# Rotating 96 images by 90 degrees: smaller first and last pieces, and first loads split over two queues

## Chip, cores and metric

The kernel runs on one core of a Trainium2 chip. The metric is the device time of one execution in microseconds (us); lower is better.

## The reference

```python
batch, c, h, w = 32, 3, 256, 256
x = np.random.randn(batch, c, h, w).astype(np.float32)

def reference(x):
    return np.rot90(x, k=1, axes=(-2, -1)).astype(np.float32)
```

Each of the 32 x 3 = 96 images of 256 x 256 float32 values (256 KB) is rotated by a quarter turn: a transposition of the image and a reversal of the order of its rows. All 25.17 MB are read once and 25.17 MB are written once; there is no arithmetic.

## The kernel before

The 96 images are taken in 6 groups of 16 (4.19 MB). A group goes through three stages:

- Two loads of 2 MB each on the sync queue (SP, line L43, queue q1 in the profile) fill a tile S of 128 partitions with 2 x 4096 float32 values each. A partition holds, for each half of the group, R = 16 whole rows of an image.
- Sixteen transposes on VectorE (DVE, L49) move S to a tile U. Each works on blocks of 32 x 32 values and handles one column offset q out of 16: 512 values per partition. The reversed strides in the source view do the reversal. The 32 columns of a block are made of 16 column positions times the 2 halves of the group, so every transpose reads both loads, and all 16 are needed before either half of U is complete.
- Two stores of 2 MB each on the scalar queue (ACT, L51, queue q10) write U to the output.

```python
src = S.rearrange("p b (r k q) -> p q r k b", r=R, q=R)[:, ::-1, :, ::-1]
dst = U.rearrange("p a (q k r) -> p q r k a", q=R, r=R)
for q in range(R):
    nc.vector.transpose(dst[:, q], src[:, q])
```

S and U come from pools of three buffers each. The loop over the groups is written out when the kernel is built, and the framework puts the semaphores in: a load of group 3 waits until the transposes of group 0 have read its buffer, a transpose of group 3 until group 0's stores have left U. Each transfer signals one of eight DMA semaphores, which are used again in turn; a transfer that takes one again waits for the transfer that had it before. Each queue issues its transfers in the order of the program. SP only issues loads, and ACT only issues stores; DVE only transposes.

Of the kernel before, what the change touches and what calls it, by code (L numbers as in the profile page):

```python
# [1 line left out]

# [4 lines left out]


@with_exitstack
def kernel(  # L10
    ctx: ExitStack,
    tc: tile.TileContext,
    x: bass.AP,
    out: bass.AP,
):
    nc = tc.nc
    B, C, H, W = x.shape
    assert H == W == 256
    N = B * C
    P = 128  # L20
    R = 16
    K = H // R
    A = 32 // K
    G = 4 * A * A
    F = R * W
    fp32 = mybir.dt.float32


    x_v = x.rearrange("b c h w -> (b c h w)").rearrange(
        "(g b a qk f) -> g b qk a f", b=A, a=A, qk=4 * K, f=F  # L30
    )

    o_v = out.rearrange("b c h w -> (b c h w)").rearrange(
        "(g b a qk f) -> g a qk b f", b=A, a=A, qk=4 * K, f=F
    )

    in_pool = ctx.enter_context(tc.tile_pool(name="in_pool", bufs=3))
    out_pool = ctx.enter_context(tc.tile_pool(name="out_pool", bufs=3))

    for g in range(N // G):  # L40
        S = in_pool.tile([P, A, F], fp32, name="S")
        for b in range(A):
            nc.sync.dma_start(out=S[:, b], in_=x_v[g, b])  # L43
        U = out_pool.tile([P, A, F], fp32, name="U")

        src = S.rearrange("p b (r k q) -> p q r k b", r=R, q=R)[:, ::-1, :, ::-1]
        dst = U.rearrange("p a (q k r) -> p q r k a", q=R, r=R)
        for q in range(R):
            nc.vector.transpose(dst[:, q], src[:, q])  # L49
        for a in range(A):  # L50
            nc.scalar.dma_start(out=o_v[g, a], in_=U[:, a])  # L51


# [1 line left out]
_INS = ['x']  # L55
_OUTS = [((32, 3, 256, 256), 'float32')]


# [23 lines left out]
```

## Time and profile before

| | |
|---|---|
| Time, median of 3 runs (lowest to highest) | 124.6 us (124.37 to 124.67) |
| Profiled execution: time, span | 124.52 us, 122.7 us |
| VectorE busy, 96 transposes | 90.7 us, 74% of the span |
| Bytes read and written in HBM | 25.17 MB and 25.17 MB |
| Mean DMA rate over the span | 410 GB/s |
| q1 (loads), q10 (stores), share of the 16 DMA engines | 48.9%, 47.9% |
| 12 loads of 2,048 KB, issue to landing | median 22.3 us |
| 12 stores of 2,048 KB, issue to landing | median 23.3 us |

The span runs from the first to the last instruction of the core, and the time of an execution is some 1.8 us longer. In the profile, rows of slices show how busy an engine is in each fortieth of the span, as a digit in tenths. A line such as "q1 hardware_dynamic" gives a queue's packets, its megabytes and the share of the 16 DMA engines' time that its packets took. The time from issue to landing includes the wait behind earlier transfers of the same queue. SPq and ACTq are the queues that issue DMAs.

### The profile page before, as it was taken

The numbers are of one execution on the slowest core, as the hardware profiler recorded it, in microseconds if no ns is written. First come the engines' busy times: TensorE is split into PE (matmuls) and PEld (weight loads), VectorE is DVE, ScalarE is ACT, GpSimd is POOL, SyncE is SP. The second block draws the span as 40 slices with busy tenths as digits, with TensorE's granted clock in tenths as the row PEclk, the third lists the DMA queues.
The fourth block names the chain that finished last, engine by engine and source line by source line (L and its number), as shares of the span: only waits on it lengthen the run. The fifth ranks groups of instructions, "written<-read, shape, count | busy, mean of one in ns | idle before, by whom it ended". The sixth has DMA issues, their size and how long they took to land.

```text
span 122.7 us, 182 instructions
## 1 busy us (share of the span) xinstructions
DVE 90.7 (74%) x96; POOL 0.2 (0%) x4
## 2 busy tenths in 40 slices
DVE  0000699999999999999999999999906999930000
POOL 0000000000000000000000000000000000000000
DMA  3999999999999999999999999999999999999992
GB/s 85 406 433 443 427 427 427 427 427 427 310 432 432 433 433 427 427 433 432 419 433 438 427 427 427 432 438 432 432 427 438 438 427 433 433 427 427 427 432 101
DMA packets 3457, 50.34 MB, mean 410 GB/s; under 512 B 384, under 2 KB 384, under 8 KB 384
## 3 DMA queue, kind: packets, MB, share of 16 engines
q1 hardware_dynamic: 1728, 25.17, 48.9%
q10 hardware_dynamic: 1728, 25.17, 47.9%
q14 instruction: 1, 0.01, 0.0%
HBM read 25.17 MB, written 25.17 MB: 410 GB/s over the span
## 4 chain that ended last, share of the span: by engine, by line
DMA 53%; DVE 31%; SPq 1%; issue 1%; DVEq 1%; ACTq 0%
DVE U L49 31%; DMA out_dram<-U 28%; DMA S<-in_x_dram 26%; SPq L43 1%; DVEq L77 1%; ACTq L51 0%; DVEq L49 0%
## 5 line engine op out<-in xcount | busy, mean ns | idle before, releaser
L49 DVE STREAM_TRANSPOSE U<-S 128x512 f32<-128x512 f32 x96 | 90.7, 1055 | 17.7 <-DMA S<-in_x_dram 13.3
L66 POOL MEMSET const-uint8-127<- 128x1 uint8 x1 | 0.1, 102 | 0.0
L66 POOL MEMSET const-bfloat16-1.0<- 128x1 bf16 x1 | 0.1, 101 | 0.0
L66 POOL MEMSET const-float32-0.0<- 128x1 f32 x1 | 0.1, 98 | 0.2 <-issue 0.2
L66 POOL MEMSET const-float32-1.0<- 128x1 f32 x1 | 0.1, 98 | 0.0
## 6 DMA issues: line engine op xcount, KB each, us to landing
S<-in_x_dram SPq DMA_DIRECT2D x12, 2048.0 KB, 22.3
out_dram<-U ACTq DMA_DIRECT2D x12, 2048.0 KB, 23.3
```

The source lines that it names most:

```text
L43: nc.sync.dma_start(out=S[:, b], in_=x_v[g, b])
L49: nc.vector.transpose(dst[:, q], src[:, q])
L66: nc = _bacc.Bacc("TRN2", target_bir_lowering=False, num_devices=1)
L77: with _tile.TileContext(nc) as tc:
```

## The change

The kernel still takes six groups of 16 images, with the same pools, and groups 1 to 4 are handled as before (lines L64, L69 and L71 in the changed kernel). The first and the last group are of another kind: each is made of 4 pieces of 4 images (1 MB).

- A partition holds R = 8 rows of one image per piece, that is 2048 values or 8 KB. 32 partitions hold a whole image, so a piece can be transposed without the others.
- One transpose instruction (L53) with an 8 x 8 x 32 access pattern does a whole piece, and one store of 1 MB (L54, scalar queue) follows it.
- The last group's pieces are loaded by one transfer each on the sync queue (L48).
- The first group's pieces are loaded by two transfers each: partitions 0 to 63 on the sync queue (L45) and partitions 64 to 127 on the scalar queue (L46), 512 KB each.

```diff
-    R = 16
-    K = H // R
-    A = 32 // K
-    G = 4 * A * A
-    F = R * W
+    G = 16
+    KINDS = [1, 2, 2, 2, 2, 1]
+    F = G * H * W // P
...
-    for g in range(N // G):
-        S = in_pool.tile([P, A, F], fp32, name="S")
-        for b in range(A):
-            nc.sync.dma_start(out=S[:, b], in_=x_v[g, b])
-        U = out_pool.tile([P, A, F], fp32, name="U")
+    for g, kind in enumerate(KINDS):
+        S = in_pool.tile([P, F], fp32, name="S")
+        U = out_pool.tile([P, F], fp32, name="U")
+        if kind == 1:
...
+            R = 8
+            Sv = S.rearrange("p (s f) -> p s f", s=4)
+            Uv = U.rearrange("p (s f) -> p s f", s=4)
+            xv = xf[g].rearrange("(s p f) -> s p f", s=4, p=P)
+            ov = of[g].rearrange("(s p f) -> s p f", s=4, p=P)
+            for s in range(4):
+                if g == 0:
+                    nc.sync.dma_start(out=Sv[:64, s], in_=xv[s, :64])
+                    nc.scalar.dma_start(out=Sv[64:, s], in_=xv[s, 64:])
+                else:
+                    nc.sync.dma_start(out=Sv[:, s], in_=xv[s])
+            for s in range(4):
...
+                src = Sv[:, s].rearrange("p (r k q) -> p q r k", r=R, q=R)[:, ::-1, :, ::-1]
+                dst = Uv[:, s].rearrange("p (q k r) -> p q r k", q=R, r=R)
+                nc.vector.transpose(dst, src)
+                nc.scalar.dma_start(out=ov[s], in_=Uv[:, s])
+        else:
...
+            R = 16
...
+            for b in range(2):
+                nc.sync.dma_start(out=Sv[:, b], in_=xv[b])
...
+            for q in range(R):
+                nc.vector.transpose(dst[:, q], src[:, q])
+            for a in range(2):
+                nc.scalar.dma_start(out=ov[a], in_=Uv[:, a])
```

More of the change, by code (lines that the diff above doesn't have):

```diff
@@ L20 @@
     P = 128
-    R = 16
-    K = H // R
-    A = 32 // K
-    G = 4 * A * A
-    F = R * W
-    fp32 = mybir.dt.float32
[L29 to L35, printed above, removed]
+    G = 16
+    KINDS = [1, 2, 2, 2, 2, 1]
+    assert len(KINDS) * G == N
+    F = G * H * W // P
+    fp32 = mybir.dt.float32
@@ L37 @@
+    xf = x.rearrange("b c h w -> (b c h w)").rearrange("(g f) -> g f", g=N // G)
+    of = out.rearrange("b c h w -> (b c h w)").rearrange("(g f) -> g f", g=N // G)
     in_pool = ctx.enter_context(tc.tile_pool(name="in_pool", bufs=3))
     out_pool = ctx.enter_context(tc.tile_pool(name="out_pool", bufs=3))
-    for g in range(N // G):
-        S = in_pool.tile([P, A, F], fp32, name="S")
-        for b in range(A):
-            nc.sync.dma_start(out=S[:, b], in_=x_v[g, b])
-        U = out_pool.tile([P, A, F], fp32, name="U")
[L46 to L51, printed above, removed]
+    for g, kind in enumerate(KINDS):
[20 more added lines that the diff above has]
+            R = 16
+            Sv = S.rearrange("p (b f) -> p b f", b=2)
+            Uv = U.rearrange("p (a f) -> p a f", a=2)
+            xv = xf[g].rearrange("(b a qk f) -> b qk a f", b=2, a=2, f=F // 2)
+            ov = of[g].rearrange("(b a qk f) -> a qk b f", b=2, a=2, f=F // 2)
+            for b in range(2):
+                nc.sync.dma_start(out=Sv[:, b], in_=xv[b])
+            src = Sv.rearrange("p b (r k q) -> p q r k b", r=R, q=R)[:, ::-1, :, ::-1]
+            dst = Uv.rearrange("p a (q k r) -> p q r k a", q=R, r=R)
+            for q in range(R):
+                nc.vector.transpose(dst[:, q], src[:, q])
+            for a in range(2):
+                nc.scalar.dma_start(out=ov[a], in_=Uv[:, a])
```

## The prediction

> **What bounds the kernel now.** I read four views, in this order: the slices of the page, the DMA answer for stretches of the trace, the same stretches as a table of windows, and the groups of instructions with their waits. The slices say which resource is full:
>
> ```profile
> DVE  0000699999999999999999999999906999930000
> ...
> DMA  3999999999999999999999999999999999999992
> GB/s 85 406 433 443 427 427 427 427 427 427 310 432 432 433 433 427 427 433 432 419 433 438 427 427 427 432 438 432 432 427 438 438 427 433 433 427 427 427 432 101
> DMA packets 3457, 50.34 MB, mean 410 GB/s; under 512 B 384, under 2 KB 384, under 8 KB 384
> ```
>
> VectorE (DVE) starts in the fifth slice and ends four slices before the end. The 16 DMA engines are busy in all slices but the ends, at 427 to 438 GB/s whatever they do. Three things fall short: the first slice (85), one in the middle (310, about 31 to 34 us) and the last (101). Who was on the engines, for 2 to 30, 36 to 90 and 93 to 118 us:
>
> ```profile
> q1 hardware_dynamic: 800, 11.80, 100.2%
> ...
> q1 hardware_dynamic: 793, 11.68, 50.6%
> q10 hardware_dynamic: 790, 11.63, 50.3%
> ...
> q10 hardware_dynamic: 739, 10.80, 100.8%
> ```
>
> q1 is the sync queue (loads), q10 the scalar queue (stores). Loads alone, an even mixture and stores alone all fill the engines. So moving stores earlier buys no rate by itself; what can be bought is time in which the engines are short of work. The windows price it (columns: stretch, length, DVE, POOL, clock, DMA share, GB/s):
>
> ```profile
> 0.00:3.00 3.00, 0.00 (x0) 0.20 (x4) 1.00 0.34 87
> ...
> 30.00:33.00 3.00, 3.00 (x4) 0.00 (x0) 1.00 0.99 333
> 33.00:36.00 3.00, 3.00 (x5) 0.00 (x0) 1.00 0.91 377
> 36.00:90.00 54.00, 52.81 (x57) 0.00 (x0) 1.00 1.01 432
> ```
>
> Against 432 GB/s, the start loses 3 x (1 - 87/432) = 2.4 us. The middle loses 3 x (1 - 333/432) + 3 x (1 - 377/432) = 0.69 + 0.38 = **1.07 us**. Payload at 432 is 50.33 MB / 432 = 116.5 us of the 122.7 us span; most of the rest is start and end latency, which no order of groups removes. In the middle dip the DMA share is 0.99 and 0.91, while the rate is down by a quarter and an eighth: packets took longer, the engines were not short of packets. It coincides with the first stores and with the first refill of S, both issued at 28.58 us:
>
> ```profile
> 28.58 1.19 SPq L43 DMA_DIRECT2D S<-in_x_dram  x2
> 28.58 1.45 ACTq L51 DMA_DIRECT2D out_dram<-U  x2
> ```
>
> DVE's size, from the timeline, is 15.20 us for a group of 16 transposes, 0.95 us each (the page's mean of 1055 ns includes overlap with the next):
>
> ```profile
> 93.14 15.20 DVE L49 STREAM_TRANSPOSE U<-S 128x512 f32<-128x512 f32 x16 [4.15 <-DMA out_dram<-U]
> ```
>
> A group costs the DMA engines 8.39 MB / 432 = 19.4 us. DVE has 4 us to spare in each.
>
> [...] No transfer of the kernel before covers half the partitions on the SBUF side[...].
>
> **The change, part by part.** Durations are of the profiled execution: span 122.7, time 124.52, so 1.82 us outside the span; it lies 0.08 under the median of 124.6, which I neglect.
>
> 1. *Issue.* The order of the built program has on the sync queue 4 half loads (L45), 8 loads of 2 MB (L64) and 4 of 1 MB (L48); on the scalar queue 4 half loads (L46) ahead of the stores: 4 of 1 MB, 8 of 2 MB, 4 of 1 MB. That is 36 DMAs for 24. An issue takes 0.6 us (604 ns median for loads). The scalar queue's 4 extra end near 0.7 + 2.4 = 3.2 us, before any store is ready; cost 0, covered by the wait for data. If that cover were gone they would delay the first store by 2.4 us.
>
> 2. *First store.* The first 2 MB landed 7.6 us after issue at 0.73, so 1 MB would land 2.4 us sooner, at about 5.9 us. Transposing a piece (L53, 128x2048) at 0.95 us per 512 elements takes 3.8 us: the first store is issued near 9.7 us, not 28.58. DVE's total stays 96 x 0.95 = 91.2 us. The 8x8x32 form isn't in the trace; bounds follow in the rivals.
>
> 3. *Does either queue run dry?* Loads alone move 3.2 MB up to 9.7 us. Then group 0's stores, in 8 KB packets against the loads' 16 KB, get a third: 4.19 MB in 29 us, to 38.8 us, with 8.4 MB loaded. Group 1 is loaded near 28 us and transposed 15.2 us later, so q10 is empty from 38.8 to 43.4 us, and loads take the whole rate (2.0 MB). The other 11.6 MB of loads share evenly, 54 us, to about 97 us. Group 3's first load waits for S of group 0, free near 20 us, and later refills for a group transposed long before. Semaphores are reused, so a load now also waits for an older transfer: group 3's second load for group 0's third store (about 31 us), group 5's third piece for group 2's first store (about 73 us). Both times q1 still holds over 2 MB, as group 2 and group 4 are still arriving. Cost 0. At 97 us 9.3 MB of stores remain, 21.5 us, while DVE needs about 12 us and the last store 2.4: the end stays full.
>
> 4. *The dip.* If it was the refill meeting a nearly drained queue, it goes: -1.07. If it is what the first stores cost whenever they come, it moves to 10 us: 0. I take -0.5.
>
> 5. *Packets of 8 KB.* Groups 0 and 5 have 1,024 more packets, 64 per engine. An 8 KB instruction fetch (q14) in a stretch of 0.4 us had a share of 4.8%: 0.048 x 16 x 0.4 = 0.307 us. A 16 KB packet is 1.008 x 16 x 25 / 659 = 0.612 (10.80 MB are 659 packets). So the overhead of one more packet is between 0 and 0.008 us: 0 to 0.5 us in sum, I take 0.25. Twelve more DMAs add 12 semaphore packets per engine, 0.1 us at a packet's 0.008.
>
> 6. *The halves.* Group 0's 4.19 MB normally take 9.7 us. Both queues hold equal bytes[...]. [...] I take the middle, **+4.85**, and keep 0 and +9.7. What sits behind it: group 1's loads behind the lower halves on q1, group 0's stores behind the upper halves on q10[...]. The loss is paid in full, because later stages have no spare DMA time. A gain below 0 is limited to quicker start-up from two issuers, under the 0.4 us that 3 to 6 us lose at 377 GB/s (another row of the windows).
>
> Sum: 124.52 - 0.5 + 0.25 + 0.1 + 4.85 = **129.2 us**.
>
> **The rivals.** *A: the halves complement each other and the dip goes.* For it: [...] q1 and q10 together already ran at 432. [...] Time: 124.52 - 1.07 + 0.35 - 0.3 (start) = 123.5, **faster**. It decides if the half stage runs above 400 GB/s: below that, 4.19/0.4 - 9.7 = 0.8 us eats the gain. *B: [...] the dip moves to 10 us.* 124.52 + 0.35 - 0.3 = 124.6, no change; the page's high DMA share in the dip speaks for slow packets at the first store, not for an empty queue. *C: strict serialization*, +9.7: 134.1[...]. *D: the new transpose form is slow.* [...] DVE starts group 5 near 93 us and must end by 117 for the end to stay full, so 6 us per piece is where it decides; at twice the known rate, 7.6 us, it ends 4 x 1.6 = 6.4 us late: 131. [...] *E: the change doesn't advance the stores.* If the scalar queue's halves lag, store 0 leaves late, up to 22 us in case C; still no dry queue, so it costs nothing of its own.
>
> **How the numbers follow.** A measurement of this kernel tells about 0.3% (0.37 us) from no change. Halves held back (the forecast through C): 0.60. A: 0.15. B: 0.22, of which 0.02 falls on slower. D: 0.03. So faster 0.15, same 0.20, slower 0.65. For slower cases alone the range is 125.5 to 134. The whole range runs from 123.9, inside A, to 133.9, just short of strict serialization; about 1 in 6 is left out.
>
> **What would show it.** Right: in the first 12 to 22 us the rate is clearly under 430 with a high DMA share (8 KB packets taking over 0.31 us each), the last half load lands after 14 us, later slices stay at 427 to 438, and DVE's first instruction is near 6 to 8 us. Step 4 shows as a dip near 10 us or none; step 2 as the first L54 issue; step 3 as no slice under 420 from 40 us on. Wrong: a rate of 430 from 4 us on, or a long idle end with DVE as the last releaser.

## The result, and the profile after

The changed kernel takes 131.62 us (median of 4 runs, 131.33 to 132.75) against 124.56 us for the kernel before (4 runs): a ratio of 1.0585, 95% interval 1.052 to 1.065. It is slower by 7.1 us, where 129.2 was forecast, inside the range. The profiled execution took 131.33 us with a span of 129.5 us.

The slices of the page of the changed kernel (3.24 us each), and its queues:

```profile
DVE  0047698930099999999999999079999999574000
...
DMA  3999999999999999999999999999999999999993
GB/s 91 223 233 253 256 250 362 422 433 420 435 420 453 422 443 415 450 410 435 450 410 433 445 415 430 435 435 410 448 425 430 420 440 420 453 435 397 425 428 137
DMA packets 4673, 50.34 MB, mean 389 GB/s; under 512 B 576, under 2 KB 576, under 8 KB 576
```

The DMA engines look as busy as before in every slice, but in the second to sixth they move only 223 to 256 GB/s. After that the rate is what it was. The deep dip in the eleventh slice before (310) has no counterpart. VectorE now starts in the third slice and has gaps; none of them matters, because the DMA engines have work all the way (share 1.01 to 1.02 from 3 to 117 us).

The windows (stretch, length, DVE busy, POOL busy, clock, DMA share, GB/s), first of the kernel after, then of the kernel before:

```profile
0.00:3.00 3.00, 0.00 (x0) 0.20 (x4) 1.00 0.23 60
3.00:21.00 18.00, 10.81 (x3) 0.00 (x0) 1.00 1.02 249
21.00:36.00 15.00, 5.66 (x3) 0.00 (x0) 1.00 1.01 429
36.00:90.00 54.00, 49.71 (x54) 0.00 (x0) 1.00 1.01 430
90.00:117.00 27.00, 24.54 (x15) 0.00 (x0) 1.00 1.02 433
```

```profile
3.00:21.00 18.00, 7.67 (x9) 0.00 (x0) 1.00 0.99 422
21.00:36.00 15.00, 15.00 (x17) 0.00 (x0) 1.00 0.99 404
```

As lost time against 432 GB/s (length x (1 - rate/432)): from 3 to 21 us 7.6 us after and 0.4 us before; from 21 to 36 us 0.1 and 1.0. The difference is +7.2 and -0.9. The other stretches add some 0.5, which makes the 6.8 us by which the spans differ.

What the packets did, from the DMA answer for 4 to 16 us of the kernel after (queue, packets, MB, share of 16 engines):

```profile
DMA packets 448, 2.91 MB, mean 242 GB/s; under 512 B 93, under 2 KB 93, under 8 KB 93
...
q10 hardware_dynamic: 238, 1.58, 55.9%
q1 hardware_dynamic: 210, 1.33, 45.8%
```

Of 448 packets 93 are under 512 B (the page has 576 of these for 36 transfers, 16 each; the prediction calls them semaphore packets); the other 355 are rows of 8 KB. The engines' time, 1.017 x 16 x 12 us, over 355 gives 0.55 us a row. In e1_full_sync, without the split, it is 0.31 (4 to 9 us: 1.023 x 16 x 5 us over 264 rows). The engines count as busy, but each row takes them longer. The two queues share about evenly.

The new transpose form is nearly as dear per element as the old one (group row: busy us, mean ns, idle before and what ended it):

```profile
L53 DVE STREAM_TRANSPOSE U<-S 128x2048 f32<-128x2048 f32 x8 | 31.4, 3957 | 13.5 <-DMA S<-in_x_dram 13.5
```

3,957 ns for 2,048 values per partition is 0.99 us for 512, against 0.95 of the old form.

### The profile page after: what moved, and what is told of

It is laid out like the page before. It is cut to its first block, busy times and chain, and to the rows that moved or that the text cites. A ratio compares the mean times of both kernels' runs of the same rounds, so it can differ in the third digit from the quotient of the medians.

```text
span 129.5 us, 183 instructions
## 1 busy us (share of the span) xinstructions
DVE 91.9 (71%) x72; POOL 0.2 (0%) x4
## 3 DMA queue, kind: packets, MB, share of 16 engines
q1 hardware_dynamic: 2048, 23.07, 45.0%
## 4 chain that ended last, share of the span: by engine, by line
DMA 63%; DVE 25%; issue 1%; ACTq 1%; SPq 0%; DVEq 0%
DMA S<-in_x_dram 48%; DVE U L69 22%; DMA out_dram<-U 15%; DVE U L53 3%; ACTq L46 1%; SPq L48 0%; DVEq L69 0%
## 5 line engine op out<-in xcount | busy, mean ns | idle before, releaser
L69 DVE STREAM_TRANSPOSE U<-S 128x512 f32<-128x512 f32 x64 | 60.6, 1052 | 12.8 <-DMA S<-in_x_dram 12.6
L53 DVE STREAM_TRANSPOSE U<-S 128x2048 f32<-128x2048 f32 x8 | 31.4, 3957 | 13.5 <-DMA S<-in_x_dram 13.5
```

The costliest lines, as they stand in the source:

```text
L53: nc.vector.transpose(dst, src)
```

## The experiments

The theory (P), an assumption of the author that the runs were to try: what counts is which partitions a transfer covers. When all of them lie in the lower half (0 to 63) or all in the upper half (64 to 127), it runs at little over half rate: 249 GB/s in the changed kernel from 3 to 21 us, 422 in the kernel before. Rivals: the small pieces and packets cost the time (Q), two queues that load at once disturb each other (T), any transfer of 64 partitions or 512 KB is slow (R). Diffs are against the changed kernel unless said otherwise.

**e1_full_sync: the split undone, pieces kept.**

```diff
-                if g == 0:
-                    nc.sync.dma_start(out=Sv[:64, s], in_=xv[s, :64])
-                    nc.scalar.dma_start(out=Sv[64:, s], in_=xv[s, 64:])
-                else:
-                    nc.sync.dma_start(out=Sv[:, s], in_=xv[s])
+                nc.sync.dma_start(out=Sv[:, s], in_=xv[s])
```

> Only the split is undone: group 0's four pieces are loaded by one 128-partition transfer each, on the sync queue. Theory P [...]: the rate from 3 to 12 us is back at 420 GB/s or more and the time falls by the 7.2 us that the half stage lost, to 124.1 +- 0.4 us. Rival Q (small pieces, 8 KB packets or the new order of stores cost the time): it stays above 129 us. For the middle dip: if it was what the first stores cost whenever they come, a slice near 10 us falls to about 310 GB/s and the time is 124.6 or more; if it was the late refill, no slice falls and the time is 123.7 to 124.2.

Measured: 124.08 us, 0.9961 of the kernel before (0.9948 to 0.9973). P holds and Q falls: the split alone costs 7.5 us, and the pieces by themselves gain 0.45. Windows of this kernel:

```profile
3.00:21.00 18.00, 15.44 (x4) 0.00 (x0) 1.00 1.02 421
21.00:36.00 15.00, 8.28 (x9) 0.00 (x0) 1.00 1.00 424
```

```profile
12.00:15.00 3.00, 3.00 (x2) 0.00 (x0) 1.00 1.00 366
```

The first stretch is back at 421. The finer window has 366 GB/s just after the first store was issued at 9.45 us. The time fits the late refill (123.7 to 124.2), but the rate does fall after the first store, though not to 310. So this run left the dip open.

**e2_full_two_queues: full width, but two queues.**

```diff
-                    nc.sync.dma_start(out=Sv[:64, s], in_=xv[s, :64])
-                    nc.scalar.dma_start(out=Sv[64:, s], in_=xv[s, 64:])
+                if g == 0 and s % 2:
+                    nc.scalar.dma_start(out=Sv[:, s], in_=xv[s])
```

> Group 0's pieces are loaded by one 128-partition transfer each, pieces 0 and 2 on the sync queue, 1 and 3 on the scalar queue: two queues load at once, but no transfer covers half the partitions. Theory P: full rate from 3 us, time within 0.5 us of the kernel with all four on the sync queue. Rival T (two queues that load at the same time disturb each other, whatever the partitions): 240 to 300 GB/s in the first 20 us and 129 us or more.

Measured: 123.93 us, 0.9956 (0.9941 to 0.9972), the fastest kernel of all, though its interval overlaps that of e1_full_sync. While both queues load, it runs at 420 GB/s:

```profile
3.00:12.00 9.00, 3.58 (x1) 0.00 (x0) 1.00 1.00 420
```

e1_full_sync has 424 in the same window. T falls: two queues that load at once do no harm here.

**e3_halves_sync: halves, but one queue.**

```diff
-                    nc.scalar.dma_start(out=Sv[64:, s], in_=xv[s, 64:])
+                    nc.sync.dma_start(out=Sv[64:, s], in_=xv[s, 64:])
```

> The halves are kept, but all eight transfers of group 0 are on the sync queue, lower half, upper half, and so on. Theory P: [...] the rate is 216 to 225 GB/s (two queues gave 249 from 3 to 21 us), group 0 takes about 19 us and the time is 133 to 134.5 us, slower than the changed kernel. Rival T (two queues loading): with one queue the loss is gone, 124 to 125 us.

Measured: 131.56 us (1.0574, 1.0552 to 1.0595), the same as the changed kernel and not 133 or more. Its windows say why the rate was as expected and the total was not:

```profile
3.00:18.00 15.00, 8.39 (x3) 0.00 (x0) 1.00 1.02 221
18.00:21.00 3.00, 3.00 (x1) 0.00 (x0) 1.00 0.98 344
```

One queue runs at 221 GB/s, slower than two at 242 (4 to 16 us above), as the author had estimated. But the scalar queue is free of loads here, so its first store (issued at 11.96 us, with packets on q10 only from 18 us on) runs beside the last half loads: q10 moved 0.61 MB from 18 to 21 us and the rate rose to 344. In the changed kernel the stores stand behind the scalar queue's half loads: its first store, issued at 12.19 us, landed 18.0 us later, here it took 12.6. The losses from 3 to 21 us come out alike, 7.9 and 7.6 us. The expectation had left that filling out.

**e4_before_halves: the split alone, on the kernel before.**

```diff
-            nc.sync.dma_start(out=S[:, b], in_=x_v[g, b])
+            if g == 0:
+                xh = x_v[g, b].rearrange("(h qk) a f -> h qk a f", h=2)
+                nc.sync.dma_start(out=S[:64, b], in_=xh[0])
+                nc.scalar.dma_start(out=S[64:, b], in_=xh[1])
+            else:
+                nc.sync.dma_start(out=S[:, b], in_=x_v[g, b])
```

> The kernel before with one part of the change alone: each of its first two 2 MB loads is split by partition halves over the sync and scalar queues (1 MB each, 16 KB packets); groups, transposes and stores are as before. Theory P: 4.19 MB at 220 to 290 GB/s instead of 430, 5 to 9 us more than before: 130 to 134 us, 16 KB packets of 0.9 to 1.2 us in that stage. Rival Q (small pieces or packets): 124.6 us, as before.

Measured: 133.98 us, 1.0766 (1.0732 to 1.0799): 9.45 us more than before, where 5 to 9 was expected; the time is within its 130 to 134. Two windows of this kernel:

```profile
3.00:24.00 21.00, 0.00 (x0) 0.00 (x0) 1.00 1.00 225
36.00:90.00 54.00, 53.85 (x58) 0.00 (x0) 1.00 1.00 418
```

From 3 to 24 us it moves 225 GB/s where the kernel before moves 424. Group 0's 4.19 MB at half of 432 GB/s would cost 9.7 us more, so with two queues and 16 KB packets the loss is nearly all of that. The packets from 3 to 21 us:

```profile
DMA packets 288, 3.93 MB, mean 218 GB/s; under 512 B 48, under 2 KB 48, under 8 KB 48
...
q1 hardware_dynamic: 160, 2.10, 53.5%
q10 hardware_dynamic: 128, 1.84, 46.4%
```

The 240 rows took 0.999 x 16 x 18 us, 1.20 us each instead of 0.61. The second window above holds a dip as well, some 1.7 us (54 x (1 - 418/432)): the first stores of this kernel are issued at 40.36 us, and from 42 to 45 us it has 289 GB/s.

**e5_middle_first and e11_middle_first_again: the middle 64 partitions first.**

```diff
-                    nc.sync.dma_start(out=Sv[:64, s], in_=xv[s, :64])
-                    nc.scalar.dma_start(out=Sv[64:, s], in_=xv[s, 64:])
+                    nc.sync.dma_start(out=Sv[32:96, s], in_=xv[s, 32:96])
...
+            if g == 0:
+                for s in range(4):
+                    nc.sync.dma_start(out=Sv[:32, s], in_=xv[s, :32])
+                    nc.sync.dma_start(out=Sv[96:, s], in_=xv[s, 96:])
```

> The changed kernel with group 0 loaded on the sync queue alone, in another cut: first the middle 64 partitions (32 to 95) of all four pieces, four transfers of 512 KB, then partitions 0 to 31 and 96 to 127 of each piece, eight transfers of 256 KB. Theory P [...] these 2.1 MB move at 420 GB/s or more, with 8 KB packets of 0.31 us, until about 7 us; the outer quarters [...] fall to 216 to 290 GB/s. Time 127 to 129.5 us, between the kernel with full loads (124.1) and the one with halves on one queue (131.6). Rival R (any transfer of 64 partitions, or of 512 KB, is slow): 216 to 250 GB/s from the start and 131 us or more.

> The kernel with the middle 64 partitions of group 0 loaded first, once more for its profile. Theory P: packets of the middle transfers take about 0.31 us (up to about 8 us), those of the outer quarters 0.5 to 0.62 us, and 127.5 to 128.8 us in all. Rival R (any transfer of 64 partitions is slow): 0.5 to 0.62 us from the start.

Measured for the first: 127.88, 128.07 and 128.74 us (ratio 1.030, 1.0263 to 1.0337), and 129.93 us in the execution that was traced. The second, the same kernel, has one execution, traced: 130.04 us, above what was expected for it. The three shorter executions have no trace, so the windows below, of the second, are of a longer one:

```profile
3.00:8.00 5.00, 0.00 (x0) 0.00 (x0) 1.00 0.98 403
9.00:17.00 8.00, 4.05 (x2) 0.00 (x0) 1.00 1.01 231
```

The middle 64 partitions, in the same 512 KB transfers with the same 8 KB rows, move at 403 GB/s, start-up included (the DMA answer has 300 packets, 54 of them small, at 97.8%: 0.978 x 16 x 5 us over 246 rows is 0.32 us each). Half loads on one queue, e3_halves_sync, have 231 in the same 5 us. The outer quarters move at 231 as well, 1.011 x 16 x 8 us over 219 rows or 0.59 us each, though these transfers are also smaller (256 KB). In the trace of e5_middle_first the middle does less well:

```profile
3.00:6.00 3.00, 0.00 (x0) 0.00 (x0) 1.00 1.02 369
```

From 3 to 6.5 us it has 353 GB/s. Both traces stay under the 420 of theory P, and why they differ is open; both lie far above the 216 to 250 of R, so R falls. What matters here is which partitions a transfer covers, not how many. Why it matters is not shown.

**e6_columns: split by columns over both queues.**

```diff
-                    nc.sync.dma_start(out=Sv[:64, s], in_=xv[s, :64])
-                    nc.scalar.dma_start(out=Sv[64:, s], in_=xv[s, 64:])
+                    nc.sync.dma_start(out=Sv[:, s, :1024], in_=xv[s, :, :1024])
+                    nc.scalar.dma_start(out=Sv[:, s, 1024:], in_=xv[s, :, 1024:])
```

> The changed kernel with each of group 0's pieces split over the sync and scalar queues by columns: 128 partitions and 4 KB of each row per transfer, 512 KB each as in the change. Theory P: [...] 415 GB/s or more from 3 us and 123.8 to 124.6 us. Rival R (transfers of 512 KB, or split pieces, are slow by themselves): under 300 GB/s and 129 us or more. The 4 KB packets add 256 packets, 16 per engine, at 0 to 0.008 us: at most 0.13 us.

Measured: 124.37 us, 0.9991 (0.998 to 1.0003):

```profile
3.00:12.00 9.00, 6.11 (x2) 0.00 (x0) 1.00 1.02 411
```

P holds in the total, though 411 is a little under the expected rate. Against e1_full_sync the split by columns costs 0.3 us, more than the 0.13 that was allowed for packets.

**e7_before_bufs4: the kernel before with early refills.**

```diff
-    in_pool = ctx.enter_context(tc.tile_pool(name="in_pool", bufs=3))
-    out_pool = ctx.enter_context(tc.tile_pool(name="out_pool", bufs=3))
+    in_pool = ctx.enter_context(tc.tile_pool(name="in_pool", bufs=4))
+    out_pool = ctx.enter_context(tc.tile_pool(name="out_pool", bufs=2))
```

> The kernel before with four buffers for S and two for U instead of three and three; all else as before. Group 3's loads can then be issued at once, ahead of the first stores at 28.6 us, and q1 holds work up to about 40 us. Dip theory 1 (late refill): no slice under 400 GB/s near 31 to 36 us and about 123.5 to 124.0 us. Dip theory 2 (first stores): the dip stays near 33 us or follows the first stores, time within 0.3 us of before unless two U buffers make VectorE wait (not on the path: the DMA engines stay full).

Measured: 137.03 us (1.1008), far from both values. Two windows of this kernel, and a line of its waits (total, times, longest, in us):

```profile
30.00:33.00 3.00, 3.00 (x4) 0.00 (x0) 1.00 1.06 382
33.00:36.00 3.00, 3.00 (x4) 0.00 (x0) 1.00 0.93 355
```

```profile
DVE U L49 <- DMA out_dram<-U: 18.7, 3, 10.8
```

Loads of group 3 were issued at 13.4 and 23.2 us, well ahead, and the dip is still there: 0.35 + 0.53 = 0.9 us. So it isn't the late refill; it comes after the first stores, issued at 28.70 us. The new time is another matter: with two U buffers VectorE waited 18.7 us for stores, and at the end the DMA engines ran out of work (89 GB/s from 99 to 108 us, 0 from 120 to 123). The remark that such waits were off the path was wrong.

**e8_first_only and e9_last_only: the pieces one end at a time** (full loads on the sync queue in both).

```diff
-    KINDS = [1, 2, 2, 2, 2, 1]
+    KINDS = [1, 2, 2, 2, 2, 2]     # e8_first_only
+    KINDS = [2, 2, 2, 2, 2, 1]     # e9_last_only
```

> Only group 0 is in pieces, all four loaded by one full transfer each on the sync queue; the last group is handled as the four in the middle. Theory: the last group's pieces bring nothing, since 9 MB of stores are still queued when its last load lands, and cost 32 more packets per engine (0.1 us) and 6 more semaphore packets: 123.9 to 124.1 us, the same as with both groups in pieces (124.08) or 0.1 us less. Rival: the pieces at the end shorten the tail, and without them it is 124.5 us, as before.

> Only the last group is in pieces (full loads on the sync queue); group 0 is handled as before. With the kernel that has only group 0 in pieces (126.8 us) it completes the table. Theory B (backlog): with late first stores a long queue of stores still covers the last group's transposes, so its pieces bring nothing: 124.5 to 124.8 us, 0.1 for packets. Rival: the pieces at the end save by themselves what the first-only kernel lost, some 2 us: 122 to 123 us.

| Groups in pieces | Time, us | Ratio to before, 95% interval |
|---|---|---|
| none (before) | 124.56 | |
| first only | 126.78 | 1.0182 (1.0166 to 1.0197) |
| last only | 124.91 | 1.0026 (1.0015 to 1.0037) |
| both (e1_full_sync) | 124.08 | 0.9961 (0.9948 to 0.9973) |

The expectation for the first failed; the second came out 0.1 above the range of theory B, and what its 0.35 us are is not shown. Timeline (in brackets VectorE's idle time before, and what ended it) and windows of the first-only kernel:

```profile
97.25 15.20 DVE L65 STREAM_TRANSPOSE U<-S 128x512 f32<-128x512 f32 x16 [4.79 <-DMA S<-in_x_dram]
```

```profile
90.00:108.00 18.00, 13.21 (x15) 0.00 (x0) 1.00 1.00 428
108.00:114.00 6.00, 4.45 (x5) 0.00 (x0) 1.00 0.49 208
```

The last group's loads land at 97 us, its sixteen transposes end at 112.5, and only then can a store of it be issued. The stores of earlier groups are gone by about 110 us, so the engines fall to 208 GB/s: 6 x (1 - 208/432) = 3.1 us lost. Early first stores use up the backlog that covered the last transposes. With pieces at the end, stores start again after 4 us and the gap closes. Each end alone loses; together they gain a little.

**e10_all_pieces: every group in pieces** (`KINDS = [1, 1, 1, 1, 1, 1]`, full loads on the sync queue).

> All six groups in pieces of 4 images, each loaded by one full transfer on the sync queue. Stores follow each piece by 4 us throughout. 2,048 more packets and 24 more DMAs than with the first and last group in pieces: per engine 128 packets at 0 to 0.008 us and 24 semaphore packets, 0.2 to 1.2 us. Theory B: the end stays full, 124.3 to 125.3 us. Rival: loads and stores of equal packets share evenly all the way and no gap at all appears, 123.5 to 124.0 us.

Measured: 124.28 us, 0.9973 (0.9959 to 0.9987): just below the range of theory B, and not in the rival's. The dip is here as well, in the windows in which e1_full_sync, with the same first group, has its own; from 15 to 18 us the rate is 426 GB/s:

```profile
9.00:12.00 3.00, 3.00 (x2) 0.00 (x0) 1.00 1.03 399
12.00:15.00 3.00, 3.00 (x2) 0.00 (x0) 1.00 0.98 347
```

## Why the prediction was right, and where it was off

- *The direction held.* The likeliest case, halves that hold each other back, is what happened. That they would was the author's estimate: no trace of the kernel before bore on it. e1_full_sync, e2_full_two_queues and e11_middle_first_again exclude the other readings that were tried. Why transfers to one half are slow is not shown. The runs show the dependence on the partitions (403 GB/s for 32 to 95, 231 for halves on one queue, both from 3 to 8 us) and a rate not far above half of 432. Half loads on two queues ran at 242 GB/s (4 to 16 us, half loads alone) against 221 on one, about a tenth more; with 16 KB packets two queues had 225.
- *Step 6 is the term that was mis-sized.* +4.85 us, the middle of 0 and +9.7 (group 0 at half of 432 GB/s), was used; the windows show +7.2 and undoing the split gains 7.5. The middle, too, was the author's estimate, from no trace. The measured rate, 242 GB/s, lies much nearer to half of 432 than to 432, and with 16 KB packets (225) next to half. The rest of the sum came near: without step 6 it gives 124.4, and e1_full_sync took 124.08. The range covered nearly all from 0 to +9.7, so a time inside it says little for taking the middle. In the changed kernel the rate rises from 233 GB/s (3 to 8 us) to 251 (12 to 18 us), while one queue has 231 and then 221. Why it rises with two queues, and why 8 KB packets gave 242 and 16 KB packets 225, was not tried and stays open.
- *Step 4 (the dip)* took -0.5. The stretch from 21 to 36 us gained 0.9, but in the changed kernel the first stores come before the half stage ends, so a dip there can't be told from that stage. e7_before_bufs4 decides between the two causes: the first stores. It moves with them (366 GB/s at 12 to 15 us in e1_full_sync) and differs in depth. What in the first stores causes it stays open.
- *Step 2:* VectorE starts at 8.19 us, 0.2 after the 6 to 8 that was given; the first store is issued at 12.19 us, not 9.7, since the half loads come late and a piece takes 3.97 us instead of 3.8. The last half load lands at 22.9 us (the sign asked for after 14). Neither delay shows as a cost of its own. Two issuers did not quicken the start: 60 GB/s up to 3 us, where the kernel before has 87 (with full loads, e2_full_two_queues has 101).
- *Step 3's cost of 0 held for this kernel, with one sign set too sharp and a wrong timetable.* The long windows from 21 to 117 us are at 429 to 433. Single slices of 397 to 415 after 40 us, which the sign excluded, stand beside slices of 440 to 453 and average out in these windows; the kernel before has a slice of 419 there itself. The last load landed at 114.2 us, not 97. Step 3's third of the rate for group 0's 8 KB rows beside 16 KB rows was an estimate; from 24 to 34 us these stores had 33.3% of the engines and the loads 67.3%. Step 3 did not apply it to the last group's 8 KB rows: from 90 to 117 us loads had 27.9% of the engines and stores 73.7%. What step 3 didn't price is how near the edge the end was; e8_first_only, with full loads and no pieces at the end, runs dry there.
- *Step 5:* from 90 to 117 us, with 8 KB loads, the rate is 433, so the small packets cost next to nothing there. e10_all_pieces, with 3 times as many more of them, is 0.2 us slower than e1_full_sync. The 0.008 us for each packet under 512 B was an estimate; no view shows it by itself.
- *The rivals.* A and B needed the halves at over 400 GB/s. C, strict serialization, gave 134.1: e4_before_halves, another kernel, came near it (133.98), this one did not. D fell: a piece takes 3.96 us against a limit of 6. At 0.99 us for 512 elements against 0.95 the new form is not faster than the old one. E happened (the first store leaves late) and cost nothing of its own.

## What to carry to other kernels

Split a load over queues by columns (124.37 us here) or by whole pieces (123.93), not by partitions 0 to 63 and 64 to 127: here that took 7 to 9.5 us longer for 4 MB. With the DMA engines full from start to end, moving the first stores forward gained almost nothing here (0.45 us with the pieces at the end, a loss of 2.2 without) and took away the backlog that hid the last group's transposes. So shorten the last group's chain in the same edit. A DMA share of 1.0 is no proof of full use (here 1.02 at 249 GB/s and 1.01 at 430): read it beside the GB/s.

## What was not expected of the hardware

- The middle 64 partitions (32 to 95) moved at 403 GB/s (3 to 8 us; 353 from 3 to 6.5 us in the other trace) and the two outer quarters at 231, in one kernel on one queue. Theory P foresaw the difference; the prediction did not speak of it.
- The first stores of a kernel come with a dip in the DMA rate at a DMA share near 1: 1.07 us in the kernel before, 0.9 in e7_before_bufs4 with loads waiting in the queue, some 1.7 in e4_before_halves, 0.4 in e1_full_sync (9 to 21 us: 415, 366, 459 and 431 GB/s in windows of 3 us). In the kernel before, no packet of a store is recorded from 28.5 to 33.3 us, though the first was issued at 28.58: it is the loads' rows that take longer (110 rows at a share of 101.5% of 4.8 us, 0.71 us each instead of 0.61).
- Half loads on two queues ran at 242 GB/s with 8 KB rows (the changed kernel, 4 to 16 us) and at 225 with 16 KB rows (e4_before_halves, 3 to 24 us).
